# Which engine awaits the last store of an average-pooling kernel: VectorE in place of SyncE

## The chip, the cores and the metric

Each run uses one core of a Trainium2 chip. The metric is device time in microseconds (us); each execution also has the profile's span, from the program's first instruction to its last. Lower is better.

## The reference

```python
def setup_inputs():
    return {"x": np.random.randn(64, 256, 8192).astype(np.float32)}

def reference(x):
    return np.mean(x, axis=2)
```

So 16384 rows of 8192 numbers, 537 MB to be read, and 64 KB to be written.

## The kernel before

SyncE streams the input through three slots of 8 MB. VectorE sums each slot along its rows; ScalarE helps only with the last rows, which come in ever smaller pieces. Results of 56 blocks are transposed by TensorE and stored early (`bulk`); the rest goes out in one small last store, which is all that is left to do after the last sum:

```python
    untracked(scaled_sum(tail_out[:, RUN - 1 : RUN], fin_in[:, 0 : lastw + k]))._wait_ge(sem, 16)
    with tc.issue_after(st.ins):
        last_store = nc.sync.dma_start(out=out_tail, in_=tail_out[:])
```

The exit block is then rebuilt by hand. SyncE awaits what everybody did except the last store; each engine drains and counts up a "gather" semaphore; GpSimd waits for the four counts and clears all semaphores but the last store's; and that one is awaited and set back by a single instruction. In the code, `wait_ge(sem, 16)` holds the engine until the count is 16, and `then_inc(sem, -16)` takes the 16 off again (in the trace of this kernel the store's sixteenth count is at 1243.910 us, the instruction runs from 1243.927 to 1243.944, and the 16 are off at 1243.944):

```python
    with nc.body("awaits", parent=parent, valid_engines=[SP]):
        for num, (name, count) in sems.items():
            if num not in stored:
                nc.sync.wait_ge(bass.SemaphoreHandle(name, num), count)
    with nc.body("clears", parent=parent, valid_engines=[SP, POOL]):
        # ... GpSimd clears the others
        for eng, num in zip((nc.sync,), stored):
            sem = bass.SemaphoreHandle(sems[num][0], num)
            eng.wait_ge(sem, 16).then_inc(sem, -16)
    # ... (the order of the exit block)
    end_bb.instructions = [
        *made["awaits"].instructions, *reports, drain, gather, *made["clears"].instructions
    ]
```

Of the kernel before, what the change touches and what calls it, by code (L numbers as in the profile page):

```python
# [19 lines left out]
def kernel(  # L20
# [5 lines left out]
    nc = tc.nc  # L26
# [162 lines left out]
    end_bb, parent = blocks[2], nc.bb_map[body_bb.name]  # L189
# [32 lines left out]
    POOL, SP = mybir.EngineType.Pool, mybir.EngineType.SP  # L222
# [3 lines left out]
    stored = [st.ins.sync_info.on_update[0].id for st in (last_store,)]  # L226
    used = sorted({*sems, *(s.num for s in (*load_sem, *tail_sem))})
    with nc.body("awaits", parent=parent, valid_engines=[SP]):
        for num, (name, count) in sems.items():
            if num not in stored:  # L230
                nc.sync.wait_ge(bass.SemaphoreHandle(name, num), count)
    with nc.body("clears", parent=parent, valid_engines=[SP, POOL]):
        rest = [n for n in range(used[0], used[-1] + 1) if n not in stored]
        while rest:
            run = [n for k, n in enumerate(rest) if n == rest[0] + k]
            nc.gpsimd.sem_clear(range(run[0], run[-1] + 1))
            rest = rest[len(run) :]
        for eng, num in zip((nc.sync,), stored):
            sem = bass.SemaphoreHandle(sems[num][0], num)
            eng.wait_ge(sem, 16).then_inc(sem, -16)  # L240
    made = {b.name: b for b in blocks}
# [39 lines left out]
```

## Time and profile before

| quantity | before |
|---|---|
| time, median of 3 | 1245.06 us (1245.02 to 1245.40) |
| profiled run: time, span | 1245.31 us, 1243.94 us |
| input moved / mean rate | 536.87 MB / 432 GB/s |
| VectorE busy | 1087.1 us, 87% |
| last store, issue to landing | 1.43 us |

The prediction below reads this profile and shows its lines. The two stretches that matter here are the last 1.5 us of the span, with the issue, the flight and the wait of an 8 KB store (SyncE's drain, at 1243.04 us, and GpSimd's clear, from 1243.15 to 1243.29 us, run during its flight), and the 1.37 us between the end of the span and the end of the time.

### The profile page before, as it was taken

The numbers are of one execution on the slowest core, as the hardware profiler recorded it, in microseconds if no ns is written. First come the engines' busy times: TensorE is split into PE (matmuls) and PEld (weight loads), VectorE is DVE, ScalarE is ACT, GpSimd is POOL, SyncE is SP. The second block draws the span as 40 slices with busy tenths as digits, with TensorE's granted clock in tenths as the row PEclk, the third lists the DMA queues.
The fourth block names the chain that finished last, engine by engine and source line by source line (L and its number), as shares of the span: only waits on it lengthen the run. The fifth ranks groups of instructions, "written<-read, shape, count | busy, mean of one in ns | idle before, by whom it ended". The sixth has DMA issues, their size and how long they took to land.

```text
span 1243.9 us, 206 instructions
## 1 busy us (share of the span) xinstructions
PE 0.6 (0%) x2; PEld 0.2 (0%) x2; DVE 1087.1 (87%) x76; ACT 16.5 (1%) x13; POOL 0.7 (0%) x6
## 2 busy tenths in 40 slices
PE   0000000000000000000000000000000000000000
PEld 0000000000000000000000000000000000000000
DVE  2898988989889889898898988989889898898988
ACT  0000000000000000000000000000000000000004
POOL 0000000000000000000000000000000000000000
DMA  9999999999999999999999999999999999999998
GB/s 436 413 432 438 438 438 432 417 432 438 438 438 438 436 413 432 438 438 438 438 436 411 434 438 438 438 438 436 411 434 438 438 438 438 434 415 432 438 438 373
DMA packets 10295, 536.95 MB, mean 432 GB/s; under 512 B 1278, under 2 KB 1590, under 8 KB 1846
## 3 DMA queue, kind: packets, MB, share of 16 engines
q1 hardware_dynamic: 10294, 536.94, 99.9%
q14 instruction: 1, 0.01, 0.0%
HBM read 536.87 MB, written 0.07 MB: 432 GB/s over the span
## 4 chain that ended last, share of the span: by engine, by line
DMA 70%; DVE 29%; issue 0%; SPq 0%; DVEq 0%
DMA xt<-in_x_dram 70%; DVE res L92 26%; DVE tail L92 3%; DVE fin_in L92 0%; SPq L82 0%; DVEq L173 0%; DVE fin_in L98 0%; DVEq L98 0%
## 5 line engine op out<-in xcount | busy, mean ns | idle before, releaser
L92 DVE TENSOR_REDUCE res<-xt 128x2 f32<-128x16384 f32 x56 | 964.4, 17222 | 139.4 <-DMA xt<-in_x_dram 139.4
L92 DVE TENSOR_REDUCE tail<-xt 128x2 f32<-128x16384 f32 (+1 forms) x7 | 112.0, 16001 | 13.8 <-DMA xt<-in_x_dram 13.8
L95 ACT ACT_TABLE_LOAD x1 | 1.3, 1283 | 1181.3 <-DVE tail L92 1181.3
L95 ACT ACTIVATE xt<-xt 128x8192 f32<-128x8192 f32 (+5 forms) x6 | 14.7, 2443 | 43.9 <-DMA xt<-in_x_dram 43.7
L92 DVE TENSOR_REDUCE fin_in<-xt 128x1 f32<-128x256 f32 (+3 forms) x5 | 5.0, 1007 | 0.4 <-DMA xt<-in_x_dram 0.4
L92 DVE TENSOR_REDUCE head<-xt 128x1 f32<-128x4096 f32 x1 | 4.4, 4420 | 0.7 <-DMA xt<-in_x_dram 0.7
L154 PE MATMUL ps<-ident,res 128*56 128x128 f32 x2 | 0.6, 404 | 1103.9 <-DVE res L92 1103.9
L95 ACT ACTIVATION_READ_ACCUMULATOR xt<-xt 128x1 f32 x6 | 1.1, 186 | 0.0
L155 DVE TENSOR_SCALAR bulk<-ps 56x128 f32<-56x128 f32 x2 | 0.5, 284 | 0.6 <-PE ps L154 0.6
L98 DVE TENSOR_SCALAR_CACHE_REDUCE fin_in<-fin_in 128x265 f32<-128x265 f32 x1 | 0.4, 430 | 0.2 <-DVE fin_in L92 0.2
L154 PEld LDWEIGHTS ps<-ident,res 128*56 128x56 f32 x2 | 0.2, 128 | 1103.9 <-issue 1103.9
L64 POOL TENSOR_SCALAR_AFFINE_SELECT ident<-ident 128x128 f32<-128x128 f32 x1 | 0.3, 294 | 0.1
L98 DVE TENSOR_SCALAR_CACHE_REDUCE head<-head 128x2 f32<-128x2 f32 x1 | 0.2, 155 | 0.1
L158 DVE TENSOR_SCALAR tail_out<-tail 128x14 f32<-128x14 f32 x1 | 0.2, 176 | 0.1
L63 POOL MEMSET ident<- 128x128 f32 x1 | 0.2, 205 | 0.3 <-POOLq L265 0.3
L265 POOL MEMSET const-bfloat16-1.0<- 128x1 bf16 x1 | 0.1, 102 | 0.0
L265 POOL MEMSET const-uint8-127<- 128x1 uint8 x1 | 0.1, 102 | 0.0
L265 POOL MEMSET const-float32-0.0<- 128x1 f32 x1 | 0.1, 99 | 0.2 <-issue 0.2
L265 POOL MEMSET const-float32-1.0<- 128x1 f32 x1 | 0.1, 99 | 0.0
L98 DVE DVE_READ_ACCUMULATOR head<-head 128x1 f32 x1 | 0.1, 82 | 0.0
L98 DVE DVE_READ_ACCUMULATOR fin_in<-fin_in 128x1 f32 x1 | 0.1, 81 | 0.0
## 6 DMA issues: line engine op xcount, KB each, us to landing
xt<-in_x_dram SPq DMA_DIRECT2D x1, 4096.0 KB, 31.1
xt<-in_x_dram SPq DMA_DIRECT2D x1, 2048.0 KB, 35.7
xt<-in_x_dram SPq DMA_DIRECT2D x1, 1024.0 KB, 37.7
xt<-in_x_dram SPq DMA_DIRECT2D x63, 40.8
xt<-in_x_dram SPq DMA_DIRECT2D x1, 512.0 KB, 38.5
xt<-in_x_dram SPq DMA_DIRECT2D x1, 256.0 KB, 38.7
xt<-in_x_dram SPq DMA_DIRECT2D x1, 128.0 KB, 38.6
fin_in<-in_x_dram SPq DMA_DIRECT2D x1, 128.0 KB, 38.4
```

Of the source, the lines that this page charges most:

```text
L63: nc.gpsimd.memset(ident[:], 0.0)
L64: nc.gpsimd.affine_select(out=ident[:], in_=ident[:], compare_op=mybir.AluOpType.not_equal, fill=1.0, base=0, pattern=[[-1, P]], channel_m ...
L92: return untracked(nc.vector.tensor_reduce(out=dst, in_=src, axis=X, op=ADD))
L95: return untracked(nc.scalar.activation(out=src, in_=src, func=COPY, accum_out=dst))
L98: return nc.vector.tensor_scalar(out=src, in0=src, scalar1=inv, scalar2=None, op0=mybir.AluOpType.mult, op1=ADD, accum_out=dst,)
L154: nc.tensor.transpose(out=ps[:TB, :], in_=res[:, r, :], identity=ident[:])
L155: nc.vector.tensor_scalar_mul(out=bulk[:TB, :, r], in0=ps[:TB, :], scalar1=inv)
L158: nc.vector.tensor_scalar_mul(out=tail_out[:, 0 : RUN - R], in0=tail[:], scalar1=inv)
L265: nc = _bacc.Bacc("TRN2", target_bir_lowering=False, num_devices=1)
```

## The change

The engine that sits in the wait for the last store is VectorE instead of SyncE. VectorE has nothing left to do by then (its exit drain ends at 1242.50 us, and the store lands at 1243.91), and the intent is to have the idle engine take the end of the work.

```diff
-    with nc.body("clears", parent=parent, valid_engines=[SP, POOL]):
+    with nc.body("clears", parent=parent, valid_engines=[POOL, mybir.EngineType.DVE]):
 ...
-        for eng, num in zip((nc.sync,), stored):
+        for eng, num in zip((nc.vector,), stored):
             sem = bass.SemaphoreHandle(sems[num][0], num)
             eng.wait_ge(sem, 16).then_inc(sem, -16)
```

## The prediction

> **What bounds the kernel now.** I read four kinds of views, from the whole to the last microsecond. First the page: what the engines and the DMA engines do in the whole span, and the chain that ended last.
>
> ```profile
> span 1243.9 us, 206 instructions
> DMA  9999999999999999999999999999999999999998
> GB/s 436 413 432 438 438 438 432 417 432 438 438 438 438 436 413 432 438 438 438 438 436 411 434 438 438 438 438 436 411 434 438 438 438 438 434 415 432 438 438 373
> DMA xt<-in_x_dram 70%; DVE res L92 26%; DVE tail L92 3%; DVE fin_in L92 0%; SPq L82 0%; DVEq L173 0%; DVE fin_in L98 0%; DVEq L98 0%
> L92 DVE TENSOR_REDUCE res<-xt 128x2 f32<-128x16384 f32 x56 | 964.4, 17222 | 139.4 <-DMA xt<-in_x_dram 139.4
> ```
>
> The reader is to see that the DMA row stands at 9 until the last slice, and that every wait of VectorE's 56 large reductions ended with a landing of input. 536.87 MB at the page's mean of 432 GB/s is 1242.8 us: the stream of input sets the time. The chain's 26% of VectorE does not say otherwise; it goes through the reduction that frees a slot, while other loads are in flight. Nothing in the diff touches this stream. So the question is only what happens after the last element of input, and that is the business of the second kind of view: the timeline of the last three microseconds, VectorE first, then SyncE.
>
> ```profile
> 1242.01 0.43 DVE L98 TENSOR_SCALAR_CACHE_REDUCE fin_in<-fin_in 128x265 f32<-128x265 f32 x1 [0.15 <-DVE fin_in L92]
> 1242.37 0.08 DVE L98 DVE_READ_ACCUMULATOR fin_in<-fin_in 128x1 f32 x1
> 1242.48 0.36 SPq L167 DMA_DIRECT2D out_dram<-tail_out  x1
> ```
>
> The last sum ends at about 1242.45, the store is issued at 1242.48. Third, the instructions of three source lines, which show the exit that the timeline leaves out (line 173 is the exit block's drains, 167 the last store, 240 the wait that the change moves).
>
> ```profile
> L173 ACTq DRAIN  x1: 537/537/537, 1241.1 to 1241.1; - x1
> L173 DVEq DRAIN  x1: 185/185/185, 1242.3 to 1242.3; - x1
> L173 SPq DRAIN  x1: 7/7/7, 1243.0 to 1243.0; - x1
> ...
> DMA to landing us min/median/max: 1.4/1.4/1.4
> ...
> L240 SPq EVENT_SEMAPHORE  x1: 17/17/17, 1243.9 to 1243.9; - x1
> ```
>
> The 1.4 us stand under line 167: the store lands 1.4 us after issue, 1242.48 + 1.43 = 1243.91, and the one SyncE instruction of line 240 runs right after it and ends the span at 1243.94. VectorE has been done since 1242.5 and does nothing. Fourth, SyncE's own waits:
>
> ```profile
> SPq L164 <- DMA xt<-in_x_dram: 37.2, 1, 37.2
> SPq L167 <- DVE fin_in L98: 0.9, 1, 0.9
> SPq L240 <- SPq L240: 0.9, 1, 0.9
> ```
>
> The last row is the wait of this case: 0.9 us, put down to its own line because only the transfer's landing ends it.
>
> **After the span.** The three runs took 1245.06 us at the median and the profiled one 1245.31, against a span of 1243.94: 1.37 us lie outside the profiled program. No view prints them, but the trace's records of semaphore counts go on. I read the ones of semaphore 2 (us from the span's start): 1104.795, 1241.782, 1243.828, 1243.872, 1244.086, 1244.130, 1244.169, 1244.203, 1244.249. Then come resets of semaphores 207 upwards from 1244.204, 156 upwards from 1244.266, 105 upwards from 1244.304, 54 upwards from 1244.308 and the lowest ones until 1244.851, and a second round of nine counts from 1245.075 to 1245.433. The first five are in the order in which the engines finish or are let through: TensorE (its drain began at 1103.9), ScalarE, GpSimd, VectorE, SyncE, and the next four go back. That reading of names is mine, from the times. So the last store's waiter still matters: SyncE's arrival at 1244.086 is followed by everything else.
>
> [...] this store, issued by SyncE, took 1.43 us, which neither waiter can shorten. [...] at the barrier ahead of the kernel, where the same instruction took:
>
> ```profile
> L265 SPq EVENT_SEMAPHORE  x1: 17/17/17, 0.7 to 0.7; - x1
> L265 ACTq EVENT_SEMAPHORE  x1: 17/17/17, 0.7 to 0.7; - x1
> L265 DVEq EVENT_SEMAPHORE  x1: 21/21/21, 0.7 to 0.7; - x1
> ```
>
> 21 over 17 is 1.24[...].
>
> **The change part by part.** The built program confirms the diff: all compute, all loads and the order on every engine are the same; one semaphore instruction (wait for 16, subtract 16) leaves the end of SyncE's exit block and stands at the end of VectorE's, after VectorE's drain. No drain, clear or store moves. GpSimd's clear needs SyncE's drain at 1243.0, as before, and skips this semaphore.
>
> 1. Until the landing: 0 ns. VectorE reaches its wait at about 1242.5 and sits 1.4 us in it; the store's issue and transfer are SyncE's and DMA's as before.
> 2. From landing to the end of the wait. Before: last count 1243.910, instruction begins at 1243.927, ends at 1243.944, so 34 ns. [...] This is all the profiled span can show: 1243.94 becomes about 1243.95.
> 3. From there to the barrier count. SyncE took 1244.086 − 1243.944 = 142 ns, ScalarE 150 (from its drain's count at 1241.632 to 1241.782). VectorE's has not been seen alone, since GpSimd's count at 1243.828 held it[...].
> 4. The barrier from there. Before, SyncE is the turning point: after its count VectorE's return count comes 44 ns later, because VectorE counted at 1243.872 and had long been ready. After, VectorE counts first and must then turn around itself. In the three clean rounds that the trace holds, VectorE's first count to its return count takes 112 + 24 = 136 ns, 113 + 23 = 136 ns and 100 + 23 = 123 ns, with SyncE's count between. So about 130 instead of 44 ns: 86 more.
> 5. The return hops, resets and second round move along unchanged: 0.
>
> Sum: 9 + 36 + 86 = 131 ns, say 0.13 us slower, 0.01% of the time.
>
> **The rivals.**
> - *A gain:* the idle VectorE would be out of its wait sooner than SyncE, which has just issued and counted. Against it: SyncE's drain was done at 1243.0, so it too sat ready for 0.9 us, and its release took only 34 ns in all. At most 34 ns could be saved there, and SyncE would have its runtime entry (142 ns) behind it early, as VectorE has now. If VectorE's entry and turnaround cost less than SyncE's 176 + 44 = 220 ns, the time falls; I allow down to 1245.0.
> - *Nothing at all:* GpSimd is the late one. It counted at 1243.828, 538 ns after its clear ended at 1243.29, only 82 ns before the landing. Were it later than the waiter, the waiter would not matter. But SyncE counted 258 ns after it, so the waiter sets the end; this rival makes 1245.1.
> - [...] TensorE took 227 ns from its count at 1104.568 to its barrier count, 85 more than SyncE, so engines do differ. That makes +0.2 to +0.3 us, 1245.4.
> - *The stream itself shifts:* no edit touches it, and I give it nothing beyond scatter.
>
> **Range and chances.** The base is uncertain by more than the effect: 1245.02, 1245.06 and 1245.40 with 1245.31 for the profiled run average 1245.20, the median of the three is 1245.06. Halfway, 1245.13, plus 0.13 gives 1245.26; I say 1245.25. For the range I take the scatter of 0.4 among those runs, and −0.1 to +0.3 for the effect: 1244.9 to 1245.6. Two per cent would be 24.9 us, some 18 times the whole part outside the span; chances 0.005 faster, 0.99 same, 0.005 slower.
>
> **What would show it right or wrong.** The stream and timeline up to the store's issue should be equal within their scatter. Line 240's semaphore instruction should be VectorE's, of 21 ns rather than 17, ending about 45 ns after the last landing; step 2 is wrong if it ends earlier than 34 ns. In the semaphore records, VectorE's count should come some 180 ns after that (step 3), SyncE's some 25 ns later, and VectorE's return count about 130 ns after its first (step 4): wrong if 44 to 70 ns. The distance from last landing to the last reset should be about 0.13 us longer than the 1244.851 − 1243.910 = 0.941 us of before. A difference of timed rounds below −0.05 us, or above +0.3 us, would make the sum wrong.

The 9 ns of step 2 and the 36 ns of step 3 scaled SyncE's 34 and 142 ns by a ratio between the engines that was assumed, not measured here. The sum came to 131 ns with them. Scaled by the 21 over 17 ns of the barrier ahead of the kernel, the two terms would be 8 and 33 ns, and the sum 127 ns (an estimate from those readings of the trace of before). The last part of step 2, the 45 and 180 ns of the criteria, and the rival of a longer exit of VectorE's rest on the same assumption.

## The result, and the profile after

| | before | after |
|---|---|---|
| median of 4 runs, us | 1245.22 (1245.02 to 1245.40) | 1245.20 (1245.04 to 1245.25) |
| profiled run: time, span, us | 1245.31, 1243.94 | 1245.25, 1243.76 |

The ratio is 0.9999, with an interval of 0.9984 to 1.0014: the same. The page of the kernel after, the same rows as in the prediction:

```profile
span 1243.8 us, 206 instructions
DMA  9999999999999999999999999999999999999998
L92 DVE TENSOR_REDUCE res<-xt 128x2 f32<-128x16384 f32 x56 | 964.4, 17221 | 139.2 <-DMA xt<-in_x_dram 139.2
```

The stream and the reductions are as they were (17221 against 17222 ns a reduction, 139.2 against 139.4 us of waiting). The timeline of VectorE's last sum and SyncE's last store, kernel after:

```profile
1241.79 0.43 DVE L98 TENSOR_SCALAR_CACHE_REDUCE fin_in<-fin_in 128x265 f32<-128x265 f32 x1 [0.15 <-DVE fin_in L92]
1242.14 0.08 DVE L98 DVE_READ_ACCUMULATOR fin_in<-fin_in 128x1 f32 x1
1242.25 0.36 SPq L167 DMA_DIRECT2D out_dram<-tail_out  x1
```

Everything stands 0.22 to 0.23 us earlier than before, the store's issue at 1242.25 instead of 1242.48. No edit lies ahead of it, so this is the scatter of the stream between two executions, and it is larger than the whole effect in question. The instruction that moved, and SyncE's own waits, kernel after:

```profile
L240 DVEq EVENT_SEMAPHORE  x1: 21/21/21, 1243.7 to 1243.7; - x1
```

```profile
SPq L164 <- DMA xt<-in_x_dram: 37.2, 1, 37.2
SPq L167 <- DVE fin_in L98: 0.9, 1, 0.9
```

SyncE's third wait of 0.9 us is gone from its list, and the instruction of line 240 is VectorE's, 21 ns instead of 17. To take the stream's scatter out, I count from the landing of the last store's last piece. The times below are nanoseconds (ns) after it, from the trace's semaphore records:

```
                                                  before   after
the waiting instruction ends (end of the span)        34      48
the count of 16 is taken off                          34      57
barrier after the span:  VectorE's first count       -38     238
                         SyncE's count               176     262
                         VectorE's return count      220     359
                         last of the four returns    339     480
last of the resets                                   941    1083
profiled time minus the landing's time              1400    1537
```

From the landing on, the kernel after is slower by 139 ns at VectorE's return count, by 142 at the last reset and by 137 ns in the device time (which is listed to 10 ns only). The landing itself came 197 ns earlier (1243.713 against 1243.910 us), so the profiled runs read 60 ns less: −197 + 137. "The same" is thus right on the time, and at the same time the exit did get slower, by about what was predicted (139 ns against 131).

### The profile page after: what moved, and what is told of

Same layout as the page of the kernel before. It is cut to its first block, busy times and chain, and to the rows that moved or that the text cites. A ratio compares the mean times of both kernels' runs of the same rounds, so it can differ in the third digit from the quotient of the medians.

```text
span 1243.8 us, 206 instructions
## 1 busy us (share of the span) xinstructions
PE 0.6 (0%) x2; PEld 0.2 (0%) x2; DVE 1087.0 (87%) x76; ACT 16.4 (1%) x13; POOL 0.7 (0%) x6
## 4 chain that ended last, share of the span: by engine, by line
DMA 70%; DVE 29%; issue 0%; SPq 0%; DVEq 0%
DMA xt<-in_x_dram 70%; DVE res L92 26%; DVE tail L92 3%; DVE fin_in L92 0%; SPq L82 0%; DVEq L173 0%; DVE fin_in L98 0%; DVEq L98 0%
## 5 line engine op out<-in xcount | busy, mean ns | idle before, releaser
L92 DVE TENSOR_REDUCE res<-xt 128x2 f32<-128x16384 f32 x56 | 964.4, 17221 | 139.2 <-DMA xt<-in_x_dram 139.2
```

The source lines that it names most:

```text
L92: return untracked(nc.vector.tensor_reduce(out=dst, in_=src, axis=X, op=ADD))
```

## The experiments

Two theories stood against each other. **Position and turnaround**: the barrier after the span goes through the engines in the order TensorE, ScalarE, GpSimd, VectorE, SyncE and back (a reading of the nine counts from 1104.795 to 1244.249 us in the trace of before), so the later in the row the waiter, the less comes after it; and VectorE needs 123 to 136 ns from its first count to its return count (three undisturbed rounds in the trace of before), which SyncE's wait used to hide. **Instruction time**, the rival of the next expectations: only VectorE's slower handling of such instructions (21 ns for the semaphore instruction, against 17 on SyncE) made the exit longer, so any engine with SyncE's 17 ns would do as well as SyncE. A third possibility was that there is no effect at all, as the first ratio says.

All results are gathered here (ns after the landing, from one profiled execution each; VectorE's return count is the point at which all kernels can be compared):

```
run                 waits      its own   VectorE's  VectorE's  last    time -
                    for store  count     1st count  return     reset   landing
before              SyncE       176       -38        220        941    1400
after               VectorE     238       238        359       1083    1537
e1_dve_again        VectorE     238       238        358       1087    1544
e10_dve_third       VectorE     239       239        360       1083    1534
e2_act_waits        ScalarE     187       269        390       1115    1566
e3_pe_waits         TensorE     319       435        556       1239    1695
e4_pool_waits       GpSimd      614       658        779       1505    1958
e5_dve_busy700      SyncE       176       -33        220        940    1394
e6_dve_busy1110     SyncE       215       192        313       1039    1490
e7_dve_busy2100     SyncE      1236      1213       1333       2055    2507
e8_dve_no_takeoff   VectorE     196       196        317       1040    1489
e9_sp_no_takeoff    SyncE       145       -31        190        911    1370
```

### The change again, twice

The kernel is the changed one, without any further edit.

> The change itself, again, with more rounds. My theory (position in the exit barrier plus VectorE's own turnaround): from the last landing of the store to VectorE's return count in the barrier after the span about 360 ns (before: 220), to the last reset about 1.08 us (before: 0.94), so about +0.14 us in every run, if the stream of input is put aside. Rival (nothing changes at the end, the rounds' 0.9999 is the truth): 220 ns and 0.94 us. In the timed rounds, the fast runs' scatter of 0.4 us is to be expected, so a ratio of 1.0001 by my theory, 1.0000 by the rival, and I doubt that the interval will part them; time minus span should, being 1.37 before: 1.46 to 1.50 by mine.

> The change itself once more on the chip of the run beside it, for the timed rounds. Both theories of the end: return count 358 ns after the landing. Timed minus span of all runs about 1.48 us, and the mean time minus the mean of before between 0.0 and +0.3 us by the scatter, +0.14 true.

Measured: return counts at 358 and 360 ns, so with the first profile three executions within 2 ns of each other, the two repeats on different chips. Timed, the medians are 1245.40 us against 1245.15 (ratio 1.0001, interval 0.9988 to 1.0015) and 1245.30 against 1245.12 (1.0001, 0.9987 to 1.0014). As expected, the rounds do not resolve it. What they do resolve is each run's time minus its span (spans are listed to 0.1 us): the kernel before has a mean of 1.35 us in 18 runs (1.32 to 1.39), the kernel after 1.50 us in 14 runs (1.44 to 1.54, the first result's four among them). The two ranges do not meet. The difference of the unrounded means, 0.14 us, is near that of the traces: 1.537 − 0.048 less 1.400 − 0.034 is 0.12, and with the two repeats it is 0.13 and 0.12. "No effect" is out.

### ScalarE and TensorE await the store

```diff
-    with nc.body("clears", parent=parent, valid_engines=[SP, POOL]):
+    with nc.body("clears", parent=parent, valid_engines=[POOL, mybir.EngineType.Activation]):
-        for eng, num in zip((nc.sync,), stored):
+        for eng, num in zip((nc.scalar,), stored):
```

For TensorE the two names are `mybir.EngineType.PE` and `nc.tensor`.

> ScalarE awaits the store and takes its count off. Position theory: ScalarE is second of five in the barrier, so from the landing 34 ns for the wait, 150 for its entry as seen before, then hops of 39 and 43 to GpSimd and VectorE, then VectorE's turnaround of 121 to 136: VectorE's return count at about 390 ns after the landing, against 220 with SyncE and 359 with VectorE; +0.17 us over before. Rival [...]: ScalarE's semaphore instruction took 17 ns as SyncE's did, so 220 to 230 ns and +0.00 to +0.01 us.

> TensorE awaits the store and takes its count off. Position theory: TensorE is first of the five; about 17 + 51 ns for the wait (its semaphore instruction took 51 ns ahead of the kernel), 227 ns for its entry as seen before, hops of 34, 39 and 43, then VectorE's turnaround of 121 to 136: VectorE's return count at 530 to 550 ns after the landing, +0.32 us over before. Rival [...]: at most the 119 ns that TensorE's own wait and entry are longer, so 340 ns and +0.12 us. The largest effect of the four, so if any is to be seen in timed rounds, it is this one: ratio 1.00026.

The moved instruction in the two traces, by its source line:

```profile
L240 ACTq EVENT_SEMAPHORE  x1: 17/17/17, 1243.8 to 1243.8; - x1
```

```profile
L240 PEldq EVENT_SEMAPHORE  x1: 51/51/51, 1243.9 to 1243.9; - x1
```

ScalarE's semaphore instruction is as short as SyncE's, and its own count comes only 11 ns later (187 against 176). Yet the return count stands at 390 ns, exactly where the position theory put it and 160 ns from where the instruction-time theory did. TensorE's comes at 556, 6 ns above the range given. The counts also settle the order, which the prediction had only inferred: between the landing and VectorE's return there are one forward count with SyncE waiting, two with VectorE, three with GpSimd, four with ScalarE and five with TensorE. In TensorE's case all are there: 319, 353, 391, 435 and 459 ns. Timed (e1 to e4 share the same nine runs of before), ScalarE's version has a median of 1245.26 us against 1245.15 (ratio 1.0000) and TensorE's 1245.60 (1.0003, interval 0.9989 to 1.0017); time minus span averages 1.55 and 1.59 us, although in TensorE's case 80 ns of the exit lie inside the span.

### GpSimd awaits the store

The same edit with `nc.gpsimd`, and `POOL` alone as valid engine.

> GpSimd awaits the store after its clear. Position theory: third of five. Its entry is the open number: 538 ns from its clear's end to its count, before. If that was the entry itself, its count comes 34 + 538 ns after the landing, and VectorE's return count 43 + 130 ns later, at about 745 ns: +0.52 us. If the clear was still at work in those 538 ns, the entry is as ScalarE's 150, and the return count comes at about 355 ns: +0.14 us. Rival [...]: 220 ns and +0.00 us if the entry is short.

```profile
L240 POOLq EVENT_SEMAPHORE  x1: 17/17/17, 1243.7 to 1243.7; - x1
```

GpSimd's count comes at 614 ns, so of the two alternatives the long entry is right: its clear had been done for over half a microsecond, and still it took 614 − 41 = 573 ns from the end of its wait to its count in the barrier, near the 538 ns of before. Why it is so long stays open. The return count, 779 ns, is 34 above the figure given. A median of 1245.81 us against 1245.15 (1.0005, interval 0.9991 to 1.0018) is the largest difference of the four. Its five runs lie between 1245.67 and 1245.94, all above the highest of the nine runs of before, 1245.65. Time minus span is 1.92 us. The prediction's rival that GpSimd might be the late one before is not borne out: there it counted at −82 ns and SyncE only at 176.

### VectorE made late while SyncE still waits

To part "who waits" from "when VectorE is ready", SyncE keeps the wait, and VectorE gets useless work after its exit drain:

```diff
-    with nc.body("clears", parent=parent, valid_engines=[SP, POOL]):
+    with nc.body("clears", parent=parent, valid_engines=[SP, POOL, mybir.EngineType.DVE]):
             eng.wait_ge(sem, 16).then_inc(sem, -16)
+        nc.vector.tensor_reduce(out=xl[:, 1, 0:1], in_=xl[:, 0, 0:1110], axis=X, op=ADD)
+        nc.vector.drain()
```

with 700, 1110 and 2100 elements.

> The kernel before (SyncE awaits), with one more reduction of 700 elements and a drain on VectorE after its exit drain, its result unused. From the rows of before (256: 420 ns, 512: 687, 1024: 1220) it takes some 880 ns, so VectorE is free about 0.48 us before the landing. Turnaround theory: VectorE has slack until about 180 + 77 ns before SyncE's count, so nothing changes: VectorE's return count 220 ns after the landing. A theory that any work on VectorE at the exit delays it: about 1100 ns.

> The same with 1110 elements, some 1310 ns: VectorE is free close to the landing, and by its entry of 180 ns its first count falls about when SyncE's does, 130 to 200 ns after the landing. SyncE still awaits the store. Turnaround theory: the return count comes 121 to 136 ns after VectorE's own first count, so 250 to 330 ns after the landing. Rival (the cost lies in who awaits the store and in the hop back from SyncE, 44 ns, whatever VectorE did before): 44 ns after SyncE's count, so 220 ns.

> The same with 2100 elements, some 2340 ns: VectorE is free about 0.98 us after the landing. Turnaround theory: VectorE's first count about 1160 to 1230 ns after the landing, SyncE's 24 ns later though it had been ready for a microsecond, the return count 97 ns after that: 1280 to 1350 ns after the landing, and the profiled run's time minus the landing's time about 2.5 us instead of 1.40. Rival (44 ns after SyncE's count): 70 ns from VectorE's first count to its return count.

The drains after the added reductions, by source line, one fence for each of the three kernels (700, 1110, 2100 elements):

```profile
L242 DVEq DRAIN  x1: 890/890/890, 1242.8 to 1242.8; - x1
```

```profile
L242 DVEq DRAIN  x1: 1317/1317/1317, 1242.7 to 1242.7; - x1
```

```profile
L242 DVEq DRAIN  x1: 2346/2346/2346, 1242.3 to 1242.3; - x1
```

The last number of a duration triple is the longest; as there is one drain each, the three numbers are equal. In the trace the drains end at −398, +34 and +1055 ns from the landing. The 0.9 us of work in the first kernel are free: 220 ns, as before, because VectorE's entry is over (−398 + 158 = −240 ns, with the 158 found below) before GpSimd, at −77 ns, lets it count. The second is the test proper. SyncE awaits the store as before and its wait ends at 34 ns as before, and the return count still moves to 313 ns, 121 ns after VectorE's own first count at 192. The rival's 220 is out. In the third the distance is 120 ns (1213 to 1333), not the rival's 70; SyncE, ready for a microsecond, counts 23 ns after VectorE, and the return follows 97 ns later. So the turnaround of VectorE is shown apart from the wait. It is also the same whoever waits: in all nine profiled executions of the table in which VectorE first counts after the landing and turns around itself, its return count follows its first count by 120 or 121 ns. Both kernels also give VectorE's entry with no semaphore in it: 192 − 34 and 1213 − 1055, both 158 ns. The entry of 180 ns in the expectations was the author's estimate; the profile after had shown 190 from the end of the wait (238 − 48), with the take-off.

### Without the take-off

The change has two halves, the wait and the taking-off of the count. Here the second half is left out, once on VectorE and once on SyncE:

```diff
-            eng.wait_ge(sem, 16).then_inc(sem, -16)
+            eng.wait_ge(sem, 16)
```

> The change without its second half: VectorE awaits the store but leaves the count of 16 on (the resets after the span include this semaphore). If the take-off costs the waiter nothing, VectorE's first count stays at 238 ns after the landing and its return count at 358 to 359. If the update of the semaphore is part of the chain (57 ns from landing to the update, where the instruction itself began at 27 and took 21), the first count comes up to 10 to 30 ns earlier.

> The kernel before without the take-off: SyncE awaits the store and leaves the count on; the resets after the span must clear it, or later executions would not wait (the output would still be checked). On VectorE the take-off cost 42 ns of the way (return count at 317 instead of 359 ns after the landing). [...] SyncE's count at about 142 ns instead of 176, VectorE's return count at about 186 instead of 220, profiled time minus landing 1.36 us instead of 1.40: the fastest of all kernels here, by 0.03 us, which the timed rounds will not resolve. Rival (only VectorE's take-off is slow): 220 ns again.

On VectorE the first count moves from 238 to 196 ns and the return from 359 to 317: the take-off costs 42 ns, more than the 10 to 30 expected. On SyncE the count moves from 176 to 145 and the return from 220 to 190, 30 ns in place of the expected 34 (the working of the 34 scaled VectorE's 42 ns by the assumed ratio; scaled by 17 over 21 ns it is 34 as well, an estimate). In both traces the records show this semaphore written once more among the resets, at 561 and 431 ns, as in every other trace but that of the kernel before, which lacks this record. The SyncE version gave correct outputs, and its profiled execution did wait: its semaphore instruction ran 17 ns after the landing, as before. The timed runs waited too: a skipped wait would have ended the span with GpSimd's clear, 0.61 us before the landing, so time minus span would be longer by some 0.5 us (an estimate from the counts above), but in all five it is 1.32 to 1.38 us. By the trace it is the shortest exit of all, 1370 ns from landing to the end of the time against 1400. Timed it is the same as before (1245.08 against 1245.12 us, ratio 1.0000, interval 0.9986 to 1.0013), and time minus span does not show the 30 ns either (1.356 against 1.357 us; with five runs and spans to 0.1 us, it could hardly). So it beats both kernels in the trace alone. It also leans on the resets that follow the program, which the kernel before did not.

## Why the prediction was right or wrong, point by point

- **The stream sets the time and is untouched:** right; the two pages agree in the DMA row, the mean rate (432 GB/s) and the reductions, and what differed (0.22 us at the store's issue) was scatter in the opposite direction.
- **Step 1, nothing until the landing:** right. The flight was 1.46 instead of 1.43 us in the first profile, but 1.43 and 1.42 in the two repeats. No run here splits the 1.43 us into parts.
- **Step 2, 9 ns more to the end of the wait:** right in sign, a little small: 48 instead of 34, so 14. The criterion given, "about 45 ns after the last landing", held.
- **Step 3, 36 ns more to the barrier count:** from the end of the wait it was 190 instead of 142 ns, so 48 more, and its inner working was wrong. The prediction scaled one entry of 142 ns by an assumed ratio. But that entry contains the take-off: 31 ns on SyncE and 42 on VectorE, by the runs without it. The ratio is also not that of the semaphore instructions, 21 over 17 ns or 1.24: from landing to count, 238 over 176 and 196 over 145 are both 1.35. What makes the rest is open.
- **Step 4, 86 ns more for VectorE's turnaround:** right in mechanism, shown by the kernels with VectorE kept busy. It measured 121 ns (against about 130 assumed), so 77 ns more than the 44 of before.
- **Step 5, the rest moves along unchanged:** right within 3 ns to the last reset. The prediction's reading of the hops, 34 to 47 ns where nobody is late, is not right: in the three undisturbed rounds the hop to SyncE took 23 or 24 ns and the one back to VectorE 100 to 113, the very numbers that its step 4 rests on.
- **The sum, 131 ns:** 14 + 48 + 77 = 139 measured, and 137 in the device time of the two profiles. Steps 2 and 3 were 17 ns too small together, step 4 was 9 too large.
- **The rivals:** the gain and the late GpSimd did not happen. A long exit of VectorE's own did not either: its entry, 148 to 158 ns without a take-off, is 37 to 47 ns longer than SyncE's 111, where that rival needed 0.07 to 0.17 us beyond the sum. The longest entry measured is GpSimd's, 573 ns.
- **The time and the range:** 1245.25 was given, 1245.20 measured. The allowance for scatter was what mattered; with a base known to 0.2 us only, the central value was hit partly by luck. The criterion of a difference between −0.05 and +0.3 us held: from the mean times, 1245.17 less 1245.215 is −0.045 in the first comparison, so by 0.005 us and by luck, and the two later ones gave +0.18 and +0.12.

## What to carry to other kernels

At the end of this program it was not the idlest engine that had best wait for the last transfer, but the one whose arrival has the least behind it: SyncE, by 0.14 us over VectorE (return counts at 220 and 359 ns) and 0.56 us over GpSimd (779 ns). An effect of 0.1 us in 1245 could not be seen in times that scatter by 0.4, but it could be measured to a few ns (358 to 360 in three executions) by counting from an event just ahead of it in the trace, here the landing of the last store. How little a better waiter could have gained is seen from the counts of before: GpSimd's came at −82 ns and VectorE's at −38, so even with no wait at all the return count would come at about −38 + 121 = 83 ns instead of 220 (an estimate), some 0.14 us earlier. And VectorE, while it was not the last, had slack up to a point: 0.9 us of extra work on VectorE cost nothing, 0.4 us more than that cost 93 ns.

## What the traces show of the exit, in numbers

- The cost of the way through the five engines and back depends on who comes last. From landing to VectorE's return count: SyncE 220 ns, VectorE 359, ScalarE 390, TensorE 556, GpSimd 779.
- In the trace of before, an undisturbed round takes 358 ns (1245.075 to 1245.433 us), and the last round ahead of the span 371 ns. Its hops are not equal: in the first of these the hop to SyncE takes 23 ns, and the one back to VectorE 100 ns, and VectorE needs 123 ns from count to count (120 in the same round of the trace of after).
- The first and the last reset lie 0.65 us apart (1244.204 to 1244.851 us), and the whole gap between the two rounds of counts is 0.83 us (1244.249 to 1245.075).
- From the end of an engine's last instruction to its barrier count: SyncE 111 ns, VectorE 148 to 158, both without a take-off; with one, SyncE 142, VectorE 190, ScalarE 150 (187 − 37), TensorE 239 (319 − 80) and GpSimd 573.
- The semaphore instruction takes 21 ns on VectorE and 17 on SyncE, a ratio of 1.24; the whole way from landing to count has VectorE over SyncE at 1.35.
- The device time: in all 12 profiled executions here it equals the time, from the span's start, of VectorE's return count in the second barrier round after the program, within 4 to 11 ns (before: 1245.31 against 1245.314; GpSimd waiting: 1245.67 against 1245.679). This is a coincidence of numbers in the traces, not something a run was made to test.
